# Four row norms transposed and stored at a time, six steps behind their squares, in place of two, three steps behind

## The chip, the core and the metric

The kernel runs on one core of a Trainium2 chip. Its time is the device time of one execution in microseconds (us), the median of three runs. In the text, PE is TensorE (PEld its weight loads), DVE is VectorE, ACT is ScalarE, POOL is GpSimd and SP is SyncE, which here only issues DMA transfers.

## The reference, cut to what matters

One encoder layer for two sequences (1024 and 2048 positions, 1024 features): a gated projection of the input, two kinds of attention side by side, an output projection and a layer norm. The change touches the second kind of attention, in which each head forms two softmax matrices and subtracts one from the other, and whose result is divided by its root mean square:

```python
logits = jnp.einsum('bqhmd,bkhmd->bhmqk', qb, kh).astype(jnp.float32) * (HEAD_DIM ** -0.5)
p = jax.nn.softmax(logits + bias[None, :, None], axis=-1)
w = p[:, :, 0] - lam * p[:, :, 1]
return jnp.einsum('bhqk,bkhe->bqhe', w.astype(vh.dtype), vh)
...
o = rms_norm(o, subln_w) * (1.0 - lambda_init)      # per query and head, over 128 elements
```

There are 4 heads; a block is 128 queries.

## The kernel before, in words

The kernel goes through three stages. Up to about 1150 us it projects the input, with the first kind of attention woven in. From there to about 1822 us runs the stage of the difference attention, called the logits stage here, and after a passage of some 50 us, called the tail, the output projection and the layer norm, which fill PE to the end.

**Slots and steps.** The logits stage has 80 units, one for each block of 128 queries of each head: first 64 of the long sequence (s = 1), then 16 of the short one (s = 0). `slot(n)` works on unit n in four steps, j = 0 to 3. In a step PE does four logits matmuls (L826, into the PSUM tile lg), six value matmuls of an older group (L882 to L884, into ac) and four transposes of an older unit's softmax row (L864, into a PSUM tile tp). The tp tiles come from a pool of two buffers and rotate. DVE adds the bias to the logits and takes the maximum (L831), ACT takes the exponential (L839), POOL subtracts one softmax from the other (L848, L850). Each transposed tile is then copied by ACT (L866, pth) and its remainder formed by DVE (L867, ptl), which also frees the tp buffer. Slots 80 to 85 finish older units while steps of the output projection (a generator, `other`) are woven in; these are the tail.

**Groups and norms.** 256 queries of a head make a group, whose value matmuls, osb copy (L887) and store to `ot` (L888) go together. In the long sequence a unit is a block of 128 queries and a group two units (32 groups); in the short one a unit is a whole group (16 groups). For each group `square_sum` runs at a step j = 1, every second slot in the long sequence and every slot in the short one: two transposes (L897), two squares with sums on ACT (L899), two small DVE operations (L903), and a power of -1/2 on POOL (L905) that leaves the norms of 2 x 128 queries in the tile f. A closure `store` is put on a list. The next step with j = 0, three steps later, takes it from the list behind its four L864: a transpose of f's two columns into a tp tile (L911, two rows), an ACT copy to fr (L913, a pool of one buffer), and a DMA to the DRAM tensor `frow` (L914, on SP's queue). `frow` is read in the output projection alone: `load_rest` loads it back, spread over all partitions, with four other loads for one block (L1029 to L1034, on SP's queue). There are 48 stores, 41 of them in the logits stage and 7 in the tail.

**What sets the order.** In slots below 80 the order on PE is that of the program text, and a scheduler orders the other engines by what is ready. In the tail all engines follow the program text. Each engine works through its own list in order: an instruction that waits holds back all that stands behind it on that engine. POOL also fills the bias window W of the next head (L759), once a head. In the tail ACT issues the stores to `ot` (L888) itself. Eight semaphores are taken in turn by the DMAs of both queues, and a DMA is issued only when the last one of its semaphore has landed; on ACT such a wait holds back all of ACT's list.

Of the kernel before, what the change touches and what calls it, by code (L numbers as in the profile page):

```python
# [11 lines left out]
F32 = mybir.dt.float32  # L12
F32R = mybir.dt.float32r
AF = mybir.ActivationFunctionType
ALU = mybir.AluOpType
# [5 lines left out]
P = 128  # L21
# [46 lines left out]
def hybrid_layer(ctx, tc, x_prompt, x_sample, c_prompt, c_sample, w_in, w_out, w_ada, b_ada, ln_g, ln_b,  # L68
                 attn_sink, lambda_q1, lambda_k1, lambda_q2, lambda_k2, subln_w, rel_bias, oh, eye,
                 y_prompt, y_sample):  # L70
    nc = tc.nc
# [3 lines left out]
    def pool(stack, name, bufs=1, space=None, side=None):  # L75
        if space is None:
            return stack.enter_context(tc.tile_pool(name=name, bufs=bufs, side=side, reuse_waits="tile"))
        if space == DRAM:
            return stack.enter_context(tc.tile_pool(name=name, bufs=bufs, space=space))
        return stack.enter_context(tc.tile_pool(name=name, bufs=bufs, space=space, side=side, reuse_waits="tile"))  # L80
# [6 lines left out]
    def tp():  # L87
        return ps_tp.tile([P, 512], F32, tag="tp", name="tp")

    def ac():  # L90
        return ps_ac.tile([P, 512], F32, tag="ac", name="ac")

    def dt_(shape, name):
        return dram.tile(shape, F32, name=name, tag=name)

    QA, KA, VA, GA, QB, KB, VB, GB, OT, OA = ([] for _ in range(10))
# [13 lines left out]
    frow = [dt_([HB, S], f"frow{s}") for s, S in enumerate(SEQS)]  # L110
    tbl = dt_([HA + HB, P, NREL], "tbl")

    ident = const.tile([P, P], F32, name="ident")
# [3 lines left out]
    mhalf = const.tile([P, 2], F32, name="mhalf")  # L117
# [270 lines left out]
    def fill(n):  # L388
        for _ in range(n):
            next(steps, None)  # L390
# [316 lines left out]
    class Views:  # L707
# [5 lines left out]
        def next(self):  # L713
            if len(self.made) < self.count:
                self.made.append(self.make())
            self.n += 1
            return self.made[(self.n - 1) % self.count]

    SMAX = max(SEQS)
    QG = 256  # L720
# [6 lines left out]
    for s in (1, 0):  # L727
        T = SEQS[s] // P
        for h in range(HB):
            for i in range(0, T, 2):  # L730
                g = len(groups_of)
                n = len(units)
# [6 lines left out]
    N = len(units)  # L739
# [5 lines left out]
    st, lst = ExitStack(), ExitStack()  # L745
# [40 lines left out]
    def prefetch(n, j):  # L786

        s, h, i, g = units[n]
        if j == 1:
            for u in units[n + 1:n + (3 if n >= EARLY - 1 else 2)]:  # L790
                if u[3] == asked[0] + 1 and (u[0] == 0 or u[3] == units[n + 1][3]):
                    load_queries(u[3])
        if n in staged and j == 2:
            stage(staged[n])
        if i == (4 if s else 2) and j == 2 and (s, h) != units[-1][:2]:
            load_head(*next_head[s, h])
        if n + 1 < N and units[n + 1][2] == 0 and j == 3:
            load_keys(*units[n + 1][:2], range(2, SEQS[units[n + 1][0]] // CH))
# [72 lines left out]
    def values(g, piece):  # L871
        s, h, i = groups_of[g]
        T = SEQS[s] // P
        G = groups_[g]
        Vt = heads[s, h][2]
        if piece == 0:
            G["O"] = ac()
        a = G["O"][:, :QG]
        for kb in range(piece * 2, piece * 2 + 2):
            kq, c = divmod(kb, 4)  # L880
            H, L = G["PT"][kq]
            nc.tensor.matmul(a, lhsT=Vt[kq][:, 0, c, :], rhs=H[:, c, :], start=(kb == 0), stop=False)  # L882
            nc.tensor.matmul(a, lhsT=Vt[kq][:, 0, c, :], rhs=L[:, c, :], start=False, stop=False)  # L883
            nc.tensor.matmul(a, lhsT=Vt[kq][:, 1, c, :], rhs=H[:, c, :], start=False, stop=(kb == T - 1))  # L884
        if piece == T // 2 - 1:
            osb = e_p.tile([P, QG], F32, tag="osb", name="osb")
            nc.scalar.copy(osb, a)  # L887
            (nc.sync if now[0] < N else nc.scalar).dma_start(out=OT[s][h][:, i * P:i * P + QG], in_=osb)  # L888
            G["osb"] = osb

    def square_sum(g):
        s, h, i = groups_of[g]
        G = groups_[g]
        ss = st_p.tile([P, 2], F32, tag="ss", name="ss")
        ot = [G["O"][:, QG + b * P:QG + (b + 1) * P] for b in range(2)]
        for b in range(2):
            nc.tensor.transpose(ot[b], G["osb"][:, b * P:(b + 1) * P], ident)  # L897
        for b in range(2):
            nc.scalar.activation(ot[b], ot[b], AF.Square, accum_out=ss[:, b:b + 1])  # L899
        f = st_p.tile([P, 6], F32, tag="f", name="f")  # L900
        nc.scalar.activation(f[:, 0:2], G["s0"], AF.Square, scale=EPS ** 0.5)
        for b in range(2):
            nc.vector.tensor_scalar(out=f[:, 2 + b:3 + b], in0=ss[:, b:b + 1], scalar1=1.0 / P,  # L903
                                    scalar2=f[:, b:b + 1], op0=ALU.mult, op1=ALU.add)
        nc.gpsimd.tensor_tensor(out=f[:, 4:6], in0=f[:, 2:4], in1=mhalf, op=ALU.pow)  # L905
        del groups_[g]

        def store():

            pf = tp()  # L910
            nc.tensor.transpose(pf[0:2, 0:P], f[:, 4:6], ident)  # L911
            fr = f_p.tile([2, P], F32, name="fr")
            nc.scalar.copy(fr, pf[0:2, 0:P])  # L913
            nc.sync.dma_start(out=frow[s][h, i * P:i * P + QG].rearrange("(b p) -> b p", p=P), in_=fr)  # L914

        stores.append(store)

    now, stores = [0], []

    def slot(n, extra, other=None):  # L920
        now[0] = n
        for j in range(4):
            if extra:
                fill(extra)
            if n < N:
                logits(n, j)
                prefetch(n, j)
            for g, piece in values_at.get(n, ()):
                if piece % 4 == j:
                    values(g, piece)  # L930
            if 0 <= n - LAG < N:
                transpose(n - LAG, j)
            if j == 1 and n in sums_at:
                square_sum(sums_at[n])
            if stores and j == 0:
                stores.pop(0)()
            if other is not None:
                next(other, None)

    st_p = pool(st, "stat", 7, side="right")  # L940
# [3 lines left out]
    with tc.manual_schedule(engines={PE}):  # L944
        for n in range(EARLY):
            slot(n, 5)
        project_until(2, 13)
# [2 lines left out]
    v_p = pool(st, "vq", 5)  # L950
    e_p = pool(st, "e", 2)
    f_p = pool(st, "fr", 1)
    for r in (r0_p, r1_p, wb_p, k_p, q_p):
        r.open(st)
    ps_lg.open(lst, space=PSUM)
# [199 lines left out]
    with tc.manual_schedule(engines={PE}):  # L1155
        for n in range(EARLY, N):
            slot(n, 0)
    lst.close()
    ps_po = pool(st, "ps_po", 4, PSUM)
    other = outputs()  # L1160
    with tc.manual_schedule(engines=ENGINES):
        for n in range(N, max(sums_at) + 1):
            slot(n, 0, other)
        for store in stores:
            store()
        for _ in other:
            pass
# [27 lines left out]
```

## Time and profile before

| | us |
|---|---|
| three runs | 2141.43, 2136.42, 2134.31 (median 2136.42) |
| the profiled execution | 2141.53 |
| its span, first to last instruction | 2139.7 |
| PE busy | 2076.0 (97%) |
| POOL, DVE, ACT busy | 1151.5, 1302.1, 1050.5 |

The span is taken from the first to the last instruction; the execution takes 1.8 us longer. The mean clock granted to TensorE was 0.992 of full speed. A row of a timeline gives the start, the duration, the engine, the line, the operation, its output and inputs, shape and count, and in brackets how long the engine sat idle before and which operation released it.

### The profile page before, as it was taken

Reading aid. Unit: us, or ns where it says so; the run is one execution under the profiler, and the core shown is the slowest. Engines: PE = TensorE matmul, PEld = TensorE weight load, DVE = VectorE, ACT = ScalarE, POOL = GpSimd, SP = SyncE. Lnnn points to the kernel's source line nnn. Section 1 sums busy time; section 2 is a strip of 40 time slices with the busy share of each in tenths; the row PEclk is TensorE's granted clock in tenths of the full one; section 3 lists DMA queues with packets and bytes.
Section 4 is the critical chain, followed back from the end, with each engine's and each line's share of the span. In section 5 each row is a group of like instructions: output and inputs, shape, how many; then the busy total and the mean of one; then the engine's idle time right before and its main releaser. Section 6 shows DMA issues by size and latency. Waiting matters only on the chain.

```text
span 2139.7 us, 32697 instructions
## 1 busy us (share of the span) xinstructions
PE 2076.0 (97%) x11645; PEld 1778.9 (83%) x11645; DVE 1302.1 (61%) x2536; ACT 1050.5 (49%) x2070; POOL 1151.5 (54%) x830
## 2 busy tenths in 40 slices
PE   7999999999999999999999999999999999799998
PEld 4777898888988888888887889988888899688886
DVE  5325224212225777677655989989989899555555
ACT  5211103011115677777634777777777799522221
POOL 3213213212124344343344888888888899577774
PEclk9999999999999999999999999999999999899999
DMA  9675635435538868788445122131221362557663
GB/s 271 178 263 176 183 126 167 131 123 136 152 120 228 202 172 212 196 208 213 142 129 156 38 81 77 38 110 50 81 77 38 96 178 90 162 141 204 195 195 102
DMA packets 327338, 312.45 MB, mean 146 GB/s; under 512 B 19126, under 2 KB 284086, under 8 KB 326792
## 3 DMA queue, kind: packets, MB, share of 16 engines
q1 hardware_dynamic: 326456, 309.72, 50.7%
q8 instruction: 92, 1.51, 0.3%
q10 hardware_dynamic: 720, 0.66, 0.1%
q14 instruction: 70, 0.57, 0.1%
HBM read 212.70 MB, written 97.60 MB: 145 GB/s over the span
## 4 chain that ended last, share of the span: by engine, by line
PE 76%; POOL 13%; DMA 4%; DVE 2%; issue 2%; ACT 1%; SPq 1%; ACTq 0%; DVEq 0%; POOLq 0%
PE pj L187 12%; PE pj L188 12%; PE pj L189 12%; PE lg L826 9%; POOL l L850 8%; PE po L1075 4%; PE po L1076 4%; PE po L1077 4%; PE tp L864 4%; POOL l L848 3%; PE lgA L608 3%; PE tp L644 3%; PE ac L882 2%; PE ac L884 2%; PE ac L883 2%; PE ac L636 2%
## 5 line engine op out<-in xcount | busy, mean ns | idle before, releaser
L187 PE MATMUL pj<-uH,wH 128*128 128x512 f32 x1040 | 419.0, 403 | 6.1 <-DVE gg L258 6.1
L189 PE MATMUL pj<-uH,wL 128*128 128x512 f32 x1040 | 407.8, 392 | 0.0
L188 PE MATMUL pj<-uL,wH 128*128 128x512 f32 x1040 | 407.4, 392 | 0.0
L218 POOL TENSOR_TENSOR wL<-wr,wH 128x1024 fp32r<-128x1024 f32 x74 | 181.9, 2460 | 418.8 <-DVE wH L216 377.5
L850 POOL TENSOR_TENSOR l<-l,l 128x1024 f32<-128x1024 f32 x160 | 382.8, 2413 | 1.8
L826 PE MATMUL lg<-kt,Q 128*128 128x512 f32 x1280 | 376.9, 416 | 2.0 <-DVE gg L258 1.4
L839 ACT ACTIVATE l<-l,nm 128x2048 f32<-128x2048 f32 (+1 forms) x192 | 330.7, 1723 | 15.8 <-DVE nm L831 15.8
L866 ACT CAST pth<-tp 128x512 fp32r<-128x512 f32 x320 | 186.2, 582 | 122.1 <-PE tp L864 114.1
L826 PEld LDWEIGHTS lg<-kt,Q 128*128 128x128 f32 x1280 | 217.9, 190 | 32.5 <-DVE nm L831 2.0
L831 DVE CUSTOM_DVE_ANT_0 l<-lg,W 128x1024 f32<-128x1024 f32 x192 | 233.1, 1214 | 11.6 <-PE lg L826 11.5
L848 POOL TENSOR_SCALAR l<-l,s 128x1024 f32<-128x1024 f32 x160 | 179.7, 1136 | 107.0 <-DVE s L844 50.9
L189 PEld LDWEIGHTS pj<-uH,wL 128*128 128x128 f32 x1040 | 195.7, 188 | 42.5
L867 DVE TENSOR_TENSOR ptl<-tp,pth 128x512 fp32r<-128x512 f32 x320 | 212.1, 686 | 28.8 <-ACT pth L866 26.0
L187 PEld LDWEIGHTS pj<-uH,wH 128*128 128x128 f32 x1040 | 196.2, 189 | 39.4 <-DVE gg L258 7.0
L188 PEld LDWEIGHTS pj<-uL,wH 128*128 128x128 f32 x1040 | 196.5, 189 | 31.1
L864 PE MATMUL tp<-ident,l 128*128 128x128 f32 x1280 | 193.5, 274 | 1.6 <-DVE ptl L867 1.4
L623 POOL TENSOR_SCALAR l<-l,rcA 128x384 f32<-128x384 f32 (+1 forms) x144 | 81.4, 584 | 190.6 <-DVE rcA L617 97.2
L882 PE MATMUL ac<-pth,vt 128*128 128x256 f32 x640 | 182.6, 285 | 0.0
L884 PE MATMUL ac<-pth,vt 128*128 128x256 f32 x640 | 181.2, 283 | 0.0
L883 PE MATMUL ac<-ptl,vt 128*128 128x256 f32 x640 | 180.8, 283 | 0.0
L831 DVE CUSTOM_DVE_ANT_0 l<-lg,W,nm 128x1024 f32<-128x1024 f32 x128 | 163.8, 1280 | 24.4 <-PE lg L826 19.9
L864 PEld LDWEIGHTS tp<-ident,l 128*128 128x128 f32 x1280 | 149.0, 141 | 3.9 <-PE lg L826 1.1
(210 smaller groups left out, 4044.7 us busy)
## 6 DMA issues: line engine op xcount, KB each, us to landing
wr<-in_w_in SPq DMA_DIRECT2D x39, 1024.0 KB
KAt<-ka SPq DMA_DIRECT2D x40, 384.0 KB
QAt<-qa SPq DMA_DIRECT2D x24, 512.0 KB
kt<-kb SPq DMA_DIRECT2D x24, 512.0 KB
Q<-qb SPq DMA_DIRECT2D x48, 256.0 KB
Q<-qb SPq DMA_DIRECT2D x96, 128.0 KB
vt<-vb SPq DMA_DIRECT2D x48, 256.0 KB
wa<-in_w_ada SPq DMA_DIRECT2D x32, 256.0 KB
```

The source lines that it names most:

```text
L187: nc.tensor.matmul(acc, lhsT=a(k), rhs=b(k), start=(k == 0), stop=False)
L188: nc.tensor.matmul(acc, lhsT=a(k), rhs=bl(k), start=False, stop=False)
L189: nc.tensor.matmul(acc, lhsT=al(k), rhs=b(k), start=False, stop=(k == KC - 1))
L826: nc.tensor.matmul(L[:, c * CH:(c + 1) * CH], lhsT=G["Q"][:, v, m, b * P:(b + 1) * P], rhs=Kt[kt0 + c][:, m, :], start=(v == 0), stop=(v = ...
L831: nc.vector.tensor_tensor_reduce(out=half, in0=L, in1=W[:, off:off + 1024], scale=1.0, scalar=nm[:, m, 0:1] if s and hf else 3e38, op0=ALU ...
L839: nc.scalar.activation(e, e, AF.Exp, bias=nm[:, m, hf:hf + 1], scale=-1.0, accum_out=sums)
L848: nc.gpsimd.tensor_scalar(out=rows[n][1][:, cs], in0=rows[n][1][:, cs], scalar1=r, scalar2=1.0, op0=ALU.mult, op1=ALU.mult)
L850: nc.gpsimd.tensor_tensor(out=row[:, cs], in0=row[:, cs], in1=rows[n][1][:, cs], op=ALU.add)
L864: nc.tensor.transpose(pt[:, c * P:(c + 1) * P], rows[n][0][:, (j * 4 + c) * P:(j * 4 + c + 1) * P], ident)
L882: nc.tensor.matmul(a, lhsT=Vt[kq][:, 0, c, :], rhs=H[:, c, :], start=(kb == 0), stop=False)
L883: nc.tensor.matmul(a, lhsT=Vt[kq][:, 0, c, :], rhs=L[:, c, :], start=False, stop=False)
L884: nc.tensor.matmul(a, lhsT=Vt[kq][:, 1, c, :], rhs=H[:, c, :], start=False, stop=(kb == T - 1))
```

## The change

The power of -1/2 goes into two of the four columns of a tile `four`, which two neighbouring groups of a head share. Only every second group puts a `store` on the list, with the step at which it falls due: six steps after its squares, which is j = 3 of the next slot. `store` transposes four columns at once, copies four rows and writes 512 contiguous words of `frow`. So 24 transposes, copies and DMAs stand where 48 stood. After the last slot eight steps of the output projection run before the last store. The test for the queue of the `ot` store is rewritten for a counter that counts steps and keeps its meaning. Behind the change the lines are six higher in the output projection (L1029 becomes L1035) and L905, L911, L913, L914 become L909, L915, L917, L918.

```diff
@@ values
-            (nc.sync if now[0] < N else nc.scalar).dma_start(out=OT[s][h][:, i * P:i * P + QG], in_=osb)
+            (nc.sync if now[0] < N * 4 else nc.scalar).dma_start(out=OT[s][h][:, i * P:i * P + QG], in_=osb)
@@ square_sum
-        f = st_p.tile([P, 6], F32, tag="f", name="f")
+        f = st_p.tile([P, 4], F32, tag="f", name="f")
...
-        nc.gpsimd.tensor_tensor(out=f[:, 4:6], in0=f[:, 2:4], in1=mhalf, op=ALU.pow)
+        c = i % 4
+        if c == 0:
+            four[0] = four_p.tile([P, 4], F32, name="four")
+        F = four[0]
+        nc.gpsimd.tensor_tensor(out=F[:, c:c + 2], in0=f[:, 2:4], in1=mhalf, op=ALU.pow)
...
             pf = tp()
-            nc.tensor.transpose(pf[0:2, 0:P], f[:, 4:6], ident)
-            fr = f_p.tile([2, P], F32, name="fr")
-            nc.scalar.copy(fr, pf[0:2, 0:P])
-            nc.sync.dma_start(out=frow[s][h, i * P:i * P + QG].rearrange("(b p) -> b p", p=P), in_=fr)
-
-        stores.append(store)
-
-    now, stores = [0], []
+            nc.tensor.transpose(pf[0:4, 0:P], F, ident)
+            fr = f_p.tile([4, P], F32, name="fr")
+            nc.scalar.copy(fr, pf[0:4, 0:P])
+            nc.sync.dma_start(out=frow[s][h, (i - 2) * P:(i + 2) * P].rearrange("(b p) -> b p", p=P), in_=fr)
+
+        if c:
+            stores.append((now[0] + 6, store))
+
+    now, stores, four = [0], [], [None]
@@ slot
-        now[0] = n
         for j in range(4):
+            now[0] = n * 4 + j
...
-            if stores and j == 0:
-                stores.pop(0)()
+            if stores and stores[0][0] <= now[0]:
+                stores.pop(0)[1]()
...
+    four_p = pool(st, "four", 2)
...
             slot(n, 0, other)
-        for store in stores:
+        for _ in range(8):
+            next(other)
+        for _, store in stores:
             store()
```

PE, the second store of the long sequence. Before, the transpose of f stands behind the L864 of a step j = 0; the waits in brackets name the engines whose semaphores it waits for.

```order
L884 MATMUL ac<-pth,vt 128x256
L864 MATMUL tp<-ident,l_11126 128x128 [waits DVE_49,PE_49,Pool_49]
L864 MATMUL tp<-ident,l_11126 128x128 x3
L911 MATMUL tp<-ident,f 2x128 [waits DVE_49,Pool_49]
L826 MATMUL lg<-kt,Q 128x512 x4
```

In the changed program a transpose of four columns stands behind the L864 of the last step (j = 3) of a slot.

```order
L884 MATMUL ac<-pth,vt 128x256
L864 MATMUL tp<-ident,l_11544 128x128 [waits DVE_49]
L864 MATMUL tp<-ident,l_11544 128x128 x3
L915 MATMUL tp<-ident,four 4x128 [waits DVE_49,PE_49,Pool_49]
L826 MATMUL lg<-kt,Q 128x512 x4
L882 MATMUL ac<-pth,vt 128x256 [waits Activation_49]
```

It has moved from the head of a slot to its end, and both forms wait for DVE as well as for POOL.

DVE, the changed program, an even slot of the long sequence, its steps j = 2 and j = 3 (L831 writes the softmax row l, L841 is a small reciprocal, L867 frees a tp buffer).

```order
L831 ISA l_11428,nm<-lg,W 128x1024
L831 ISA nm 128x1
L841 RECIPROCAL s_11386<-s_11386 128x1
L831 ISA l_11428,nm<-lg,W,nm 128x1024
L831 ISA nm 128x1
L867 TENSOR_TENSOR ptl<-tp,pth 128x4x128 x2
```

The same six rows stand in the program before (l_11434 in place of l_11428); DVE's list has both L867 of the last two steps behind the second L831 there, and what the change adds is a PE instruction that waits for the first of the two.

SP, the queue at the end of the logits stage, before (L1029 to L1034 are the loads of one output block).

```order
L914 DMA frow_102<-fr 2x128
L1029 DMA l_19022<-ot_98 128x4x128
L1030 DMA l_19022<-frow_103 128x4x128
L1031 DMA l_19022<-gb_97 128x4x128
L1032 DMA l_19022<-oa_99 128x4x128
L1034 DMA vt<-in_x_sample 128x1024
L914 DMA frow_102<-fr 2x128
```

And in the changed program:

```order
L918 DMA frow_102<-fr 4x128
L1035 DMA l_18936<-ot_98 128x4x128
L888 DMA ot_81<-osb 128x256
L1036 DMA l_18936<-frow_103 128x4x128
L1037 DMA l_18936<-gb_97 128x4x128
L1038 DMA l_18936<-oa_99 128x4x128
L1040 DMA vt<-in_x_sample 128x1024
L918 DMA frow_102<-fr 4x128
```

The store ahead of the first load is an older one now, and an `ot` store stands behind that load where it stood ahead of the queue's part shown before.

## Rows read from the trace of the kernel before

**Rows 1.** The page's first part: busy time, share of the span and instructions of PE.

```profile
PE 2076.0 (97%) x11645; PEld 1778.9 (83%) x11645; DVE 1302.1 (61%) x2536; ACT 1050.5 (49%) x2070; POOL 1151.5 (54%) x830
```

**Rows 2.** Windows of 50 us: busy time of each engine with its instructions, then the granted TensorE clock, the DMA share and GB/s. The first lies in the logits stage, the second reaches into the tail, the third lies in the output projection.

```profile
1300.00:1350.00 50.00, 49.77 (x336) 44.94 (x335) 45.80 (x88) 39.60 (x67) 42.60 (x26) 1.00 0.20 61
...
1800.00:1850.00 50.00, 42.99 (x293) 39.05 (x292) 39.91 (x80) 40.57 (x100) 38.07 (x27) 0.93 0.38 110
...
2000.00:2050.00 50.00, 50.00 (x217) 40.51 (x217) 27.27 (x47) 12.00 (x19) 37.81 (x33) 1.00 0.65 195
```

**Rows 3.** The timeline of all engines around one regular store of the long sequence (1308 to 1324 us).

```profile
1309.66 4.77 POOL L850 TENSOR_TENSOR l<-l,l 128x1024 f32<-128x1024 f32 x2
...
1312.73 1.18 PE L826 MATMUL lg<-kt,Q 128*128 128x512 f32 x4
...
1314.40 0.69 POOL L905 TENSOR_TENSOR f<-f,mhalf 128x2 f32<-128x2 f32 x1
...
1315.15 0.08 PEld L911 LDWEIGHTS tp<-ident,f 128*2 128x2 f32 x1 [0.33 <-POOL f L905]
...
1315.18 1.18 PE L826 MATMUL lg<-kt,Q 128*128 128x512 f32 x4
...
1317.26 1.18 PE L826 MATMUL lg<-kt,Q 128*128 128x512 f32 x4
```

**Rows 4.** The instructions of line L911 from 1180 to 1820 us: their count, and until what PE or PEld sat idle ahead of them (us, times).

```profile
L911 PE MATMUL tp<-ident,f x41: 270/271/372, 1190.8 to 1815.3; 128*2 128x128 f32 x41
...
  POOL f L905: 31.8, 37
```

**Rows 5.** The instructions of line L914 over the whole span: who waited for them (us, times).

```profile
  ACT fr L913: 5.1, 1
```

**Rows 6.** The timeline of PE around the four latest stores of the logits stage, ahead of each of which POOL had filled W; the last stands at the passage from the long to the short sequence.

```profile
1274.46 1.18 PE L826 MATMUL lg<-kt,Q 128*128 128x512 f32 x4
...
1279.22 0.37 PE L911 MATMUL tp<-ident,f 128*2 128x128 f32 x1 [2.43 <-POOL f L905]
1279.25 2.05 PE L826 MATMUL lg<-kt,Q 128*128 128x512 f32 x4
...
1282.81 1.18 PE L826 MATMUL lg<-kt,Q 128*128 128x512 f32 x4
...
1420.81 0.27 PE L911 MATMUL tp<-ident,f 128*2 128x128 f32 x1 [2.44 <-POOL f L905]
...
1560.64 0.27 PE L911 MATMUL tp<-ident,f 128*2 128x128 f32 x1 [2.19 <-POOL f L905]
...
1701.60 0.27 PE L911 MATMUL tp<-ident,f 128*2 128x128 f32 x1 [3.36 <-POOL f L905]
1701.63 1.41 PE L826 MATMUL lg<-kt,Q 128*128 128x512 f32 x4
...
1704.82 1.61 PE L826 MATMUL lg<-kt,Q 128*128 128x512 f32 x4
```

**Rows 7.** The timeline of all engines at the last step of an even slot of the long sequence and the start of the next slot, where before no store stands.

```profile
1319.35 1.17 PE L826 MATMUL lg<-kt,Q 128*128 128x512 f32 x4
...
1320.56 1.28 DVE L831 CUSTOM_DVE_ANT_0 l<-lg,W,nm 128x1024 f32<-128x1024 f32 x1 [0.17 <-PE lg L826]
...
1321.07 0.60 PE L864 MATMUL tp<-ident,l 128*128 128x128 f32 x4
...
1321.42 1.18 PE L826 MATMUL lg<-kt,Q 128*128 128x512 f32 x4
...
1321.77 1.28 DVE L867 TENSOR_TENSOR ptl<-tp,pth 128x512 fp32r<-128x512 f32 x2
```

**Rows 8.** The timeline of the short sequence: PE around a store of the last slots, and DVE and PE at the last step of a slot.

```profile
1743.59 1.18 PE L826 MATMUL lg<-kt,Q 128*128 128x512 f32 x4
...
1745.77 1.18 PE L826 MATMUL lg<-kt,Q 128*128 128x512 f32 x4
...
1820.62 0.69 DVE L867 TENSOR_TENSOR ptl<-tp,pth 128x512 fp32r<-128x512 f32 x1 [0.17 <-ACT pth L866]
...
1821.45 0.60 PE L864 MATMUL tp<-ident,l 128*128 128x128 f32 x4
```

**Rows 9.** The timeline of SP, ACT and PE in the tail (SPq is SP's queue), in order of time.

```profile
1824.45 0.24 SPq L914 DMA_DIRECT2D frow<-fr  x1
1824.80 0.37 SPq L1029 DMA_DIRECT2D l<-ot  x1
...
1838.37 0.59 ACT L866 CAST pth<-tp 128x512 fp32r<-128x512 f32 x1 [3.56 <-DMA ot<-osb]
...
1839.82 0.37 PE L911 MATMUL tp<-ident,f 128*2 128x128 f32 x1 [3.84 <-DVE ptl L867]
...
1849.60 0.38 SPq L1029 DMA_DIRECT2D l<-ot  x1
...
1862.07 0.72 ACT L1016 ACTIVATE wo<-kt,wsub 128x512 fp32r<-128x512 f32 x1 [8.05 <-DMA l<-gb]
...
1866.74 0.37 PE L911 MATMUL tp<-ident,f 128*2 128x128 f32 x1 [6.49 <-POOL f L905]
...
1872.35 0.27 PE L911 MATMUL tp<-ident,f 128*2 128x128 f32 x1 [1.00 <-POOL f L905]
```

**Rows 10.** The chain that ended last, in the tail: start, duration, what.

```profile
1850.58 11.02 DMA l<-gb
```

## The prediction

> **What bounds the kernel now.** I read the page's busy times first: PE works for 2076.0 us, 97% of the span [rows 1]. The windows say where the rest lies. In a regular stretch of the logits stage PE is busy 49.77 us of 50, in the output projection 50.00, in the window that reaches into the tail 42.99, at a granted clock of 0.93 [rows 2]. So PE bounds the logits stage and the output projection, and the tail is bound by something else. A change to other engines' small work counts only where PE waits for it, or where it adds work to PE.
>
> The timeline shows such a wait. The regular step, from one group of logits matmuls to the next, is 1317.26 - 1315.18 = 2.08 us; the step that ends in a store is 1315.18 - 1312.73 = 2.45 us, 0.37 longer. In front of the store's transpose PE's loads sit idle 0.33 us until POOL has written f [rows 3]. POOL's power starts at 1314.40, when the two L850 before it, 4.77 us long, have left the engine: it is POOL's order that makes f late, not the power's 0.69 us. The instructions of L911 in the logits stage, 41, together saw 31.8 us of such idle time in 37 cases [rows 4]; a long gap stands there once on PE and once on its load side, so I count by steps instead.
>
> **What the change removes.** In the short sequence a store that waits for nothing makes its step 1745.77 - 1743.59 = 2.18 us [rows 8]: 0.10 us is the bare price of a transpose on PE. By steps, the 41 stores of the logits stage cost: 26 regular ones of the long sequence at 0.37, 9.6 us; four late ones, behind a filling of W, with gaps of 2.43, 2.44, 2.19 and 3.36 [rows 6], each with 0.28 around the gap (1279.25 - 1274.46 - 2.08 - 2.43), 11.5 us; eleven of the short sequence at 0.10, 1.1 us. That is 22.2. After two of the four late ones the clock had fallen: the step from 1279.25 to 1282.81 took 3.56, 1.48 too long, that from 1701.63 to 1704.82 took 3.19, 1.11 too long [rows 6]. Together 24.8 us.
>
> Six steps are at least 12.5 us between squares and store instead of 6.2. The latest power came 3.36 us after PE asked for it, so with 6.2 us more it is in time everywhere: none of these waits for POOL is left. The 48 powers on POOL stay, and so does the work on DVE. The copies and DMAs that go cost nothing now: ACT and SP have room, and the only wait that the 48 DMAs caused is one of 5.1 us on ACT in the tail [rows 5]. The Trainium skill ("DMA: Bandwidth & Descriptors", anatomy of one DMA) gives a DMA a fixed cost of about 2.0 us; by it 24 fewer would be worth 48 us if they stood on the path, which the one wait of rows 5 speaks against.
>
> **What it adds.** 20 transposes of four rows in the logits stage at 0.10 each, 2.0 us, as the transpose of two rows: the matrix streamed through PE has 128 columns in both. And a wait that isn't there now. The store takes a tp buffer of the two that rotate. At j = 3 it is the one of step j = 2, and that is free when DVE has done that step's L867. In an even slot of the long sequence the order of DVE has both L867 of j = 2 and j = 3 behind the L831 of j = 3. The rows of such a slot: logits of j = 3 from 1319.35, L831 at 1320.56 for 1.28, the two L867 from 1321.77 for 1.28 together, so the first ends near 1322.43. PE's transposes of j = 3 stand at 1321.07, and the next logits start at 1321.42 [rows 7]: there the store would stand, and would wait from 1321.42 to about 1322.48, 1.05 us. Before, at j = 0, it met a buffer that was long free, and the wait for f hid it. Fourteen of the stores stand at such a place: 14 x 1.05 = 14.7 us. In the short sequence the L867 of j = 2 ends at 1821.31, before the last transposes of j = 3 at 1821.45 [rows 8]: no wait for the other six. Sum of the logits stage: -24.8 + 2.0 + 14.7 = -8 us. The bounds of the wait: nothing, if the scheduler's order or PE's lead differs a little there; up to 1.7, if both L867 must be through.
>
> **The tail.** Two waits of PE stand out, 3.84 us at 1839.82 and 6.49 at 1866.74, both at a store, and 1.00 at 1872.35 [rows 9]. Stores are only the place: the first follows ACT, which held back its copy L866 for 3.56 us until an `ot` store had landed, the second an ACT that stood 8.05 us until the load l<-gb had landed [rows 9], a load that took 11.02 us [rows 10]. These loads are late because SP works in order: the first group of loads starts at 1824.80, right behind the `frow` store of 1824.45, which had waited for its transpose; a later group starts at 1849.60 in the same way [rows 9]. After the change the first group stands behind older stores and can start when the buffer is free, near 1822, about 2.7 us earlier, and the later ones move up with it. The landing times move with the starts, as far as the DMA engines' load allows. So the first wait of PE should lose 2.7 of its 3.84 us, and with it the half clock that follows (I take 1.5 us, as after 1279 [rows 6]); the second should lose about as much as the groups move, 4 to 5 of 6.49, and the third all of its 1.00. That is 2.7 + 1.5 + 4 + 1 = 9 us. Bounds: 3, if only the starved stores themselves go and the landings stay; 12, if all three waits go. Behind the tail PE is full to the end, so what is won there is kept.
>
> Sum: -8 - 9 = -17 us. The profiled execution took 2141.53; its 17 us less are 2124.5. It was the slowest of those shown; against the median of 2136.42 the forecast is 2119.
>
> **The rivals.** *The buffer's wait does not show* (DVE is through in time, or the order differs): the logits stage gives 23 us, the sum is -32, the time 2104 to 2106. For it speaks that DVE is busy 45.80 of 50 us and so has slack [rows 2]; against it that the rows put L867 behind L831 in every even slot.
>
> *The tail gives back little*: the DMA engines are the limit there, the loads start earlier and land no earlier. For it speaks the 11.02 us for a load of 256 KB [rows 10], far longer than its issue; against it that in the window that holds the first of these loads the DMA engines were busy for a share of 0.38 only [rows 2]. Sum -8 - 3 or -8 alone, time 2126 to 2130.
>
> *The new waits cost the clock* (slower). Each of the fourteen is a gap of 1.05 us in a PE that otherwise has none. A gap of 2.43 was followed by a step of 3.56 us, one of 2.44 by none, and the 26 of 0.33 by none [rows 3, 6]. If each of the fourteen were followed by such a step, 1.48 x 14 = 21 us would come on top: +4, 2140; with clock losses over more than one step up to 2.6 each, 36 us: +19, 2156. It decides against the change from 17 / 14 = 1.2 us for each, and shows as slower from 1.7. The Trainium skill ("TensorE: Matmul & The Clock Gate", on a second failure mode, with PSUM buffers cycled) says that frequent short idles of PE between groups of matmuls that cycle through PSUM buffers can make the clock go back and forth, which is this case; the trace's 26 regular gaps do not show it, at a third of the length.
>
> *The waits only change their place*: a PE freed of the waits for f runs into POOL or DVE, so that nothing is won in the logits stage and the tail keeps its path. POOL is busy 42.60 and DVE 45.80 of 50 [rows 2], so there is room for the 8 us; I give it little: time 2132 to 2138.
>
> **How the numbers follow.** The chances: the forecast (2111 to 2126) 0.60, no wait for the buffer 0.10, little from the tail 0.15, the clock 0.08, no gain 0.07. A measurement of this kernel can tell about 0.3% from no change, 6.4 us: faster is below 2130.0, slower above 2142.8. Faster hold the first three, 0.85 less a little for the edge of the third: 0.84. The clock's rival is half between and half above: slower 0.05, the same 0.11. The range 2104 to 2131 holds the first three cases and leaves out the last two, 0.15.
>
> **What would show it.** In the profile of the changed kernel: the idle time in front of L915 released by DVE (L867) and not by POOL, near 1.05 us, fourteen times in the long sequence and next to nothing in the short one; regular steps of 2.08 where L911 stood, and after the fillings of W no gap; the granted clock at 1.00 in the logits stage; the first load of the output projection 2 to 3 us ahead of its old place, the first output matmul about 5 us earlier against the end of the logits stage, and the wait behind the load l<-gb down to one or two us. The prediction is wrong if L915 waits for `four` or for the ACT copy, if the fourteen waits are followed by half-clock matmuls, or if the wait in the tail keeps its length because the transfers and not their starts set it.

## The result, and the profile after

The changed kernel takes 2120.34 us (median; 2118.73 to 2122.41), the kernel before, timed beside it, 2138.13. The ratio is 0.992, with a 95% interval of 0.990 to 0.994: 13 to 22 us faster. The forecast was 2119, range 2104 to 2131.

The windows of the changed kernel answer to [rows 2]; the columns are the same, from the stretch and its length through the busy times of the engines to the granted clock, the DMA share and GB/s.

```profile
1250.00:1300.00 50.00, 49.06 (x335) 44.84 (x335) 45.25 (x87) 38.69 (x64) 43.67 (x28) 1.00 0.42 128
1300.00:1350.00 50.00, 48.14 (x326) 43.71 (x325) 44.87 (x87) 39.14 (x65) 42.90 (x27) 1.00 0.13 41
1790.00:1840.00 50.00, 42.70 (x307) 38.74 (x306) 40.05 (x74) 38.14 (x96) 39.19 (x27) 1.00 0.43 121
1840.00:1865.00 25.00, 21.49 (x96) 17.36 (x95) 9.19 (x18) 7.53 (x22) 16.10 (x15) 0.93 0.52 151
2000.00:2050.00 50.00, 50.00 (x219) 40.75 (x218) 27.54 (x48) 12.07 (x19) 37.77 (x33) 1.00 0.65 192
```

In a window of 50 us that holds one store PE is busy 49.06 us, in one that holds two 48.14; before it was 49.77 in a window without a late store. The output projection is full as it was. The clock stands at 1.00 in the logits stage; the window that reaches into the tail has 1.00 where before it had 0.93, and the 25 us behind it, the tail's end, 0.93.

The timeline of all engines of the changed kernel around a store in an even slot of the long sequence answers to [rows 3, 7]:

```profile
1311.83 1.28 DVE L831 CUSTOM_DVE_ANT_0 l<-lg,W,nm 128x1024 f32<-128x1024 f32 x1 [0.23 <-PE lg L826]
...
1312.34 0.60 PE L864 MATMUL tp<-ident,l 128*128 128x128 f32 x4
...
1313.04 1.28 DVE L867 TENSOR_TENSOR ptl<-tp,pth 128x512 fp32r<-128x512 f32 x2
...
1313.84 0.08 PEld L915 LDWEIGHTS tp<-ident,four 128*4 128x4 f32 x1 [1.14 <-issue]
1313.87 0.27 PE L915 MATMUL tp<-ident,four 128*4 128x128 f32 x1 [0.93 <-DVE ptl L867]
...
1313.89 1.17 PE L826 MATMUL lg<-kt,Q 128*128 128x512 f32 x4
```

The transposes of j = 3 begin at 1312.34 and PE could go on 0.35 us later, as in every step. It goes on at 1313.87, when the first of the two L867 behind the second L831 has ended. The instructions of L915 between 1180 and 1700 us (count; until what PE or PEld sat idle ahead of them, in us and times) answer to [rows 4]:

```profile
L915 PE MATMUL tp<-ident,four x15: 269/269/273, 1209.3 to 1696.2; 128*4 128x128 f32 x15
...
  issue: 16.0, 14
  DVE ptl L867: 13.1, 14
```

POOL no longer stands among the releasers. Fourteen of the fifteen waited for DVE. Counted by steps, each of the fourteen takes 3.27 to 3.28 us against 2.08 for a step without a store, and the others 2.18 to 2.19: 0.10 for the transpose, 1.10 for the wait. In a regular stretch that is a loss, one store at 1.20 us for two at 0.37, as the busy times of the windows show; the logits stage is shorter because the four late waits behind the fillings of W are gone, and the low clock behind them.

Where the time went, by three marks that every kernel here has on PE: the first L897, the last L826, and the fiftieth matmul of the first of the three output lines (L1075 before, L1081 after). The first stretch is the logits stage from its first squares on, the second the tail, the third the output projection. "Median" is the timed one; the stretches are of the one profiled execution.

| kernel | first L897 at | logits stage | tail | rest | median |
|---|---|---|---|---|---|
| before | 1183.8 | 636.7 | 77.7 | 241.6 | 2138.1 |
| before once more (e8) | 1177.0 | 633.9 | 77.6 | 241.6 | 2134.9 |
| changed | 1178.7 | 627.3 | 70.9 | 240.0 | 2120.3 |
| e1 seven steps | 1179.2 | 612.0 | 72.0 | 240.0 | 2104.2 |
| e2 single, six steps | 1179.5 | 644.9 | 74.1 | 240.4 | 2140.8 |
| e3 change in the tail alone | 1179.1 | 632.4 | 71.8 | 240.0 | 2124.4 |
| e4 change in the logits stage alone | 1180.2 | 627.4 | 75.6 | 240.0 | 2124.9 |
| e5 pairs, three steps | 1182.0 | 630.1 | 73.9 | 240.0 | 2126.9 |
| e6 single, seven steps | 1180.1 | 614.2 | 81.6 | 242.1 | 2119.9 |
| e7 seven steps, ot stores on SP | 1177.3 | 612.0 | 62.2 | 240.0 | 2094.3 |
| e9 changed, ot stores on SP | 1176.1 | 627.3 | 63.0 | 240.0 | 2109.9 |
| e10 before, ot stores on SP | 1180.6 | 631.7 | 78.8 | 241.2 | 2134.9 |
| e11 as e10, four places for fr | 1177.7 | 635.3 | 64.9 | 241.2 | 2121.2 |

The kernel before was timed again beside each set of experiments, at 2133 to 2134 us; an experiment's ratio is to that. The changed kernel was not timed again; against these later times its 2120.34 is 13 to 14 us less, and not 18.

The logits stage gave 9.4 us between the two profiles (6.6 against the second profile of before), the tail 6.8, the rest 1.6. The 5.1 us ahead of the first L897 are not the change's (e8 below). Three more kernels have the logits stage of before (e3, e10, e11) and took 632.4, 631.7 and 635.3 us for it, so a stretch of a single profile is good to a few us.

In the tail the changed kernel has these rows in the timelines of SP, ACT and PE, which answer to [rows 9]:

```profile
1807.66 0.37 SPq L1035 DMA_DIRECT2D l<-ot  x1
...
1823.76 0.59 ACT L866 CAST pth<-tp 128x512 fp32r<-128x512 f32 x1 [4.00 <-DMA ot<-osb]
...
1825.12 0.66 PE L864 MATMUL tp<-ident,l 128*128 128x128 f32 x4 [2.84 <-DVE ptl L867]
...
1844.53 0.72 ACT L1022 ACTIVATE wo<-kt,wsub 128x512 fp32r<-128x512 f32 x1 [7.61 <-DMA l<-gb]
...
1847.36 0.69 PE L897 MATMUL ac<-ident,osb 128*128 128x128 f32 x2 [3.51 <-ACT osb L887]
```

Counted from the last L826, which starts at 1820.49 before and at 1806.04 after, the first load comes at 1.6 us where it came at 4.3. But ACT is held 4.00 and 7.61 us where it was held 3.56 and 8.05, each time ahead of an `ot` store that it is to issue (L888). PE's two long waits are 2.84 and 3.51 us in place of 3.84 and 6.49, and neither stands at a store.

The chain that ended last names the transfers that ACT waited for. Before (the second is in [rows 10]):

```profile
1828.36 9.57 DMA ot<-osb
```

And in the changed kernel:

```profile
1813.41 9.90 DMA ot<-osb
...
1833.25 10.82 DMA l<-gb
```

The first is the `ot` store that ACT itself issued before: counted from the last L826 it starts at 7.9 us before and at 7.4 after, and lands at 17.4 and 17.3. The second is a load: it starts at 30.1 and 27.2 and lands at 41.1 and 38.0. So a hold of the same length can end earlier, as the second does.

The tail as one window (from the last L826 to the fiftieth output matmul), before and in the changed kernel:

```profile
1820.49:1898.16 77.67, 63.16 (x346) 53.59 (x345) 40.88 (x68) 34.63 (x91) 49.01 (x40) 0.91 0.54 150
...
1806.04:1876.94 70.90, 60.09 (x343) 51.15 (x342) 40.38 (x68) 33.67 (x88) 49.89 (x40) 0.98 0.58 165
```

PE sits idle for 14.5 us before and for 10.8 after. That is 3.7 of the 6.8 us; the other 3.1 are busy time, of three matmuls fewer at a granted clock of 0.98 in place of 0.91.

### The profile page after: what moved, and what is told of

It reads as the page before. It is cut to its first block, busy times and chain, and to the rows that moved or that the text cites. A ratio compares the mean times of both kernels' runs of the same rounds, so it can differ in the third digit from the quotient of the medians.

```text
span 2116.9 us, 32562 instructions
## 1 busy us (share of the span) xinstructions
PE 2059.4 (97%) x11621; PEld 1769.6 (84%) x11621; DVE 1300.3 (61%) x2536; ACT 1045.9 (49%) x2046; POOL 1151.1 (54%) x830
## 4 chain that ended last, share of the span: by engine, by line
PE 87%; DMA 5%; DVE 4%; ACT 1%; POOL 1%; issue 1%; SPq 1%; ACTq 0%; DVEq 0%; POOLq 0%
PE lg L826 14%; PE pj L187 12%; PE pj L188 12%; PE pj L189 12%; PE tp L864 6%; PE po L1083 4%; PE po L1082 4%; PE po L1081 4%; PE ac L882 3%; PE ac L884 3%; PE ac L883 3%; PE lgA L608 3%; PE tp L644 3%; PE ac L636 2%; PE ac L635 1%; DVE l L831 1%
## 5 line engine op out<-in xcount | busy, mean ns | idle before, releaser
L826 PE MATMUL lg<-kt,Q 128*128 128x512 f32 x1280 | 374.8, 414 | 2.1 <-DVE gg L258 1.4
L839 ACT ACTIVATE l<-l,nm 128x2048 f32<-128x2048 f32 (+1 forms) x192 | 330.9, 1724 | 15.8 <-DVE nm L831 15.8
L831 DVE CUSTOM_DVE_ANT_0 l<-lg,W 128x1024 f32<-128x1024 f32 x192 | 233.5, 1216 | 21.4 <-PE lg L826 21.3
L826 PEld LDWEIGHTS lg<-kt,Q 128*128 128x128 f32 x1280 | 217.1, 189 | 31.9 <-DVE nm L831 2.0
L867 DVE TENSOR_TENSOR ptl<-tp,pth 128x512 fp32r<-128x512 f32 x320 | 210.7, 686 | 17.8 <-ACT pth L866 16.4
L864 PE MATMUL tp<-ident,l 128*128 128x128 f32 x1280 | 192.0, 272 | 5.8 <-DVE ptl L867 5.8
L831 DVE CUSTOM_DVE_ANT_0 l<-lg,W,nm 128x1024 f32<-128x1024 f32 x128 | 164.0, 1281 | 20.9 <-PE lg L826 15.7
L864 PEld LDWEIGHTS tp<-ident,l 128*128 128x128 f32 x1280 | 147.9, 140 | 8.2 <-DVE ptl L867 5.0
```

The lines of the kernel that those rows point to most:

```text
L826: nc.tensor.matmul(L[:, c * CH:(c + 1) * CH], lhsT=G["Q"][:, v, m, b * P:(b + 1) * P], rhs=Kt[kt0 + c][:, m, :], start=(v == 0), stop=(v = ...
L831: nc.vector.tensor_tensor_reduce(out=half, in0=L, in1=W[:, off:off + 1024], scale=1.0, scalar=nm[:, m, 0:1] if s and hf else 3e38, op0=ALU ...
L839: nc.scalar.activation(e, e, AF.Exp, bias=nm[:, m, hf:hf + 1], scale=-1.0, accum_out=sums)
L864: nc.tensor.transpose(pt[:, c * P:(c + 1) * P], rows[n][0][:, (j * 4 + c) * P:(j * 4 + c + 1) * P], ident)
L867: nc.vector.tensor_tensor(out=L[:, :, qs], in0=p3, in1=H[:, :, qs].bitcast(F32), op=ALU.subtract)
```

## The experiments

**e1: one step later.** The store falls due at j = 0 of the slot after, where the buffer of j = 3 is next.

```diff
-            stores.append((now[0] + 6, store))
+            stores.append((now[0] + 7, store))
```

> The changed kernel with the store due seven steps after the squares (j = 0 of the slot after next) in place of six. Theory (the wait of L915 is for the tp buffer of step j = 2, behind DVE's L831): at j = 0 the store takes the buffer of j = 3, whose L867 ends some 0.45 us before; the fourteen steps of 3.28 us become 2.18 each, 14 x 1.1 = 15.4 us less, the time about 2105. Rival (the wait is the price of a transpose of POOL's tile, wherever it stands, or DVE's order follows the store): the steps stay near 3.3 and the time near 2120.

Measured: 2104.18 us, ratio 0.987 (0.985 to 0.989). All 20 steps with a store in the logits stage take 2.18 to 2.19 us. The timeline of all engines around one of them:

```profile
1310.24 1.28 DVE L867 TENSOR_TENSOR ptl<-tp,pth 128x512 fp32r<-128x512 f32 x2
...
1311.62 0.60 PE L864 MATMUL tp<-ident,l 128*128 128x128 f32 x4
...
1312.06 0.27 PE L915 MATMUL tp<-ident,four 128*4 128x128 f32 x1
...
1312.09 1.18 PE L826 MATMUL lg<-kt,Q 128*128 128x512 f32 x4
```

The order of DVE is as before, both L867 behind the L831 of j = 3; they end at 1311.52, the store is reached at 1311.97 and waits for nothing. The logits stage is 15.3 us shorter than the changed kernel's, as the wait for the tp buffer says (14 x 1.1 = 15.4). The time is 16 us lower by the two medians, and 12 by what each is below the kernel before beside it, as the two were timed in different sets.

**e2: the lateness without the pairing.** Each group has its own `four` and a store of two rows, six steps behind its squares.

```diff
         c = i % 4
-        if c == 0:
+        pair = False
+        w = 4 if pair else 2
+        if c == 0 or not pair:
             four[0] = four_p.tile([P, 4], F32, name="four")
         F = four[0]
+        if not pair:
+            c = 0
...
-            nc.tensor.transpose(pf[0:4, 0:P], F, ident)
+            nc.tensor.transpose(pf[0:w, 0:P], F[:, 0:w], ident)
...
-        if c:
+        if c or not pair:
             stores.append((now[0] + 6, store))
```

> The changed kernel without the pairing: 48 stores of two rows, each six steps after its squares. Theory: all stores of the long sequence in the logits stage, about 30, stand at j = 3 of an even slot and wait 1.1 us, twice as many as after the change; some 16 x 1.2 = 19 us more in the logits stage than in the changed kernel, the time about 2139, as slow as before. Rival (the lateness alone is the gain, the pairing saves nothing but 20 x 0.1): about 2123.

Measured: 2140.82 us, ratio 1.0036 (1.0023 to 1.0049): slower than before. The instructions of its store's transpose between 1180 and 1700 us:

```profile
L919 PE MATMUL tp<-ident,four x29: 269/269/273, 1193.3 to 1697.0; 128*2 128x128 f32 x29
...
  DVE ptl L867: 26.2, 28
```

Twenty-eight waits in place of fourteen, each step 3.27 to 3.28 us, and a logits stage 17.6 us longer than the changed kernel's. So the wait costs the same each time, and the lateness alone loses more than the waits for POOL cost: it pays only because the pairing halves its price. The clock does not fall behind any of the 28: the granted clock from 1190 to 1700 us is 1.00.

**e3 and e4: the two halves of the change.** In e3 only the groups of the last two heads of the short sequence are paired and late, in e4 all others; the rest store as before. Both keep the eight output steps ahead of the last store.

```diff
e3, against e2
-        pair = False
+        pair = s == 0 and h >= 2
...
-            stores.append((now[0] + 6, store))
+            stores.append((now[0] + (6 if pair else 3), store))
...
e4, against e3
-        pair = s == 0 and h >= 2
+        pair = s == 1 or h < 2
```

> The kernel before, with pairs and six steps only for the last two heads of the short sequence, whose stores lie in the tail. Theory (the tail's gain comes from its own queue order): the logits stage stays at its 637 us from the first L897 to the last L826, the stretch from the last L826 to the fiftieth output matmul falls from 77.7 to 71 us, the time is about 2131. Rival (the tail gains because of the logits stage ahead of it): 77 us there, the time about 2138.

> The changed kernel with single stores three steps after the squares for the last two heads of the short sequence, as before the change: only the logits stage has pairs. Theory: the logits stage takes 627 us as after the change, the tail to the fiftieth output matmul 77 to 78 as before; the time is about 2127. Rival (the tail follows the logits stage): the tail 71, the time 2120.

Measured: e3 2124.35 us, ratio 0.9956 (0.9940 to 0.9972), 9 us below the kernel before beside it; e4 2124.91, 0.9962 (0.9947 to 0.9977), also 9 us. Added, the halves make 18 us, as the whole did; but that was timed against a slower kernel before (13 to 14 us against the one timed here), and the 1.6 us of the column "rest" are in both halves. So the sum shows that each half gains, and not that nothing else does. The logits stage of e4 is that of the changed kernel (627.4 us), its tail 75.6 us; the tail of e3 is 71.8, near the changed kernel's 70.9. The timeline of PE in the tail of e4 has the two waits of before at their old places, with nearly their old lengths; the third, 1.00 at the last store, is gone, with the eight output steps that e4 keeps:

```profile
1826.78 0.37 PE L919 MATMUL tp<-ident,four 128*2 128x128 f32 x1 [3.75 <-DVE ptl L867]
...
1852.93 0.37 PE L919 MATMUL tp<-ident,four 128*2 128x128 f32 x1 [5.78 <-POOL four L913]
```

e3's time came out 7 us lower than the number expected: the kernel before was itself timed 4.5 us lower in this set, and e3's logits stage was 632.4 us and not 637, as the waits behind the fillings of W differ between executions (e8).

**e5: the pairing without the lateness.**

```diff
-            stores.append((now[0] + 6, store))
+            stores.append((now[0] + 3, store))
```

> The changed kernel with the store of a pair due three steps after the second squares (j = 0 of the next slot), where the stores stood before: pairing without the lateness. Theory: half of the waits for POOL go and half stay, with all four late ones (their groups are second of a pair), and no wait for the tp buffer shows; the steps that hold a store stay at 2.45 to 5.7 us in the long sequence; first L897 to last L826 about 631 us (637 less 15 x 0.37 and 6 x 0.1); the time, with some of the tail's gain, 5 to 9 us below before. Rival (pairing alone takes the wait away): 612 us there.

Measured: 2126.90 us, ratio 0.9965 (0.9951 to 0.9978), a logits stage of 630.1 us: the theory's 631. The steps with a store stay at 2.45 to 2.48 us, the late ones at 3.9 to 6.1; one of these on the timeline of PE:

```profile
1413.58 0.27 PE L915 MATMUL tp<-ident,four 128*4 128x128 f32 x1 [2.56 <-POOL four L909]
1413.61 1.18 PE L826 MATMUL lg<-kt,Q 128*128 128x512 f32 x4
```

The store waits for POOL as before, half as often.

**e6: seven steps without the pairing.** The kernel of e2 with seven in place of six.

```diff
-        stores.append((now[0] + 6, store))
+        stores.append((now[0] + 7, store))
```

> The kernel of e1 (seven steps) without the pairing: 48 stores of two rows. Theory (a store that meets a free buffer and a finished f costs PE its bare 0.10 us): first L897 to last L826 614 us, 2 us above e1, all steps with a store at 2.18; the time 2 to 6 us above e1, the tail with its 7 stores included. Rival (the pairing matters by itself, for copies and DMAs): 10 us or more above e1.

Measured: 2119.91 us, ratio 0.9935 (0.9916 to 0.9955), 16 us above e1. In the logits stage the theory holds: 614.2 us, 2.2 more than e1 for 20 more stores, 0.11 each. So 20 copies and 20 DMAs more cost nothing there. The rest of the difference, 9.6 us in the tail and 2 behind it, was not expected: by its number (10 us or more) the rival is right, in the tail alone. Two of PE's rows and two of ACT's from the timelines of the tail:

```profile
1815.88 0.37 PE L919 MATMUL tp<-ident,four 128*2 128x128 f32 x1 [6.03 <-DVE ptl L867]
...
1814.42 0.59 ACT L866 CAST pth<-tp 128x512 fp32r<-128x512 f32 x1 [5.81 <-DMA ot<-osb]
...
1869.87 0.26 ACT L921 COPY fr<-tp 2x128 f32<-2x128 f32 x1 [15.82 <-DMA frow<-fr]
...
1874.49 0.79 PE L1085 MATMUL po<-W,Q 128*128 128x512 f32 x1 [6.34 <-ACT vt L1125]
```

ACT is held 5.8 us by an `ot` store, and 15.8 us at a copy to fr (L921) until the last `frow` store has left fr. There is one fr, and its store stands on SP's queue behind the loads. Behind the first hold PE waits 6.03 us (2.86 in e1), behind the second 6.34 (none in e1): together 9.5 us more.

**e7: the stores to ot off ACT.** The kernel of e1 with them on SP's queue in the tail as well.

```diff
-            (nc.sync if now[0] < N * 4 else nc.scalar).dma_start(out=OT[s][h][:, i * P:i * P + QG], in_=osb)
+            nc.sync.dma_start(out=OT[s][h][:, i * P:i * P + QG], in_=osb)
```

> The kernel of e1 with the stores to ot issued on SP's queue in the tail too, in place of ACT's. Theory (what starves PE in the tail is ACT held back by such a store, 3.9 and 7.7 us): both holds leave ACT, PE's waits of 2.9 and 3.6 us shrink, the stretch from the last L826 to the fiftieth output matmul falls from 72 to about 67 us and the time by 3 to 5 us against e1. Rival (SP held by the same wait keeps back the loads behind it): 72 us or more and no gain.

Measured: 2094.30 us, ratio 0.981 (0.980 to 0.983), 10 us below e1, twice what was expected, with a tail of 62.2 us. Of the 9.8 us that the tail is shorter than e1's, 6.8 are idle time of PE (3.6 in place of 10.4); the rest is busy time, at a granted clock of 1.00 in place of 0.95 over the tail. PE's longest wait in it on PE's timeline is this one, which the kernels with ACT's stores have too:

```profile
1796.27 0.66 PE L864 MATMUL tp<-ident,l 128*128 128x128 f32 x4 [1.05 <-DVE ptl L867]
```

This is the fastest version.

**e8: the kernel before once more.** No edit.

> The kernel before once more, for a second profile. Theory (the first 5 us of the difference between the two profiles, ahead of the first L897, is no effect of the change): first L897 at 1179 to 1180 us as in all changed kernels; the gaps ahead of the four late stores differ between executions by up to 1.5 us, first L897 to last L826 632 to 637 us. Rival: first L897 at 1184 again.

Measured: 2134.93 us, ratio 1.0003 (0.9992 to 1.0013). The first L897 comes at 1177.0, and in all other profiles at 1176.1 to 1182.0: the 5 us ahead of it differ between executions and are no effect of the change. The steps with the late stores take 4.30, 4.09, 3.84 and 5.92 us where the first profile had 4.79, 4.79, 4.54 and 5.72. The instructions of L911 between 1170 and 1815 us:

```profile
  POOL f L905: 27.0, 34
```

That was 31.8 in [rows 4]. By steps, the 41 with a store in the logits stage take 105.8 us here and 108.2 there, which is most of the 2.8 us between the two logits stages.

**e9 and e10: what the tail's gain rests on.** The edit of e7 in the changed kernel (e9) and in the kernel before (e10).

> The changed kernel (six steps) with the stores to ot on SP's queue in the tail too. Theory (the holds of ACT at these stores starve PE in the tail, and the logits stage is independent): the stretch from the last L826 to the fiftieth output matmul falls from 70.9 us to 61 to 63, the logits stage stays at 627; the time about 2110, 10 us below the changed kernel. Rival (the gain of e7 needs the store at seven steps): 70 us, 2119.

> The kernel before with the stores to ot on SP's queue in the tail too. Theory (the change's gain in the tail is a shorter effect of the same holds of ACT): the tail falls from 77.6 us to about 64 to 67, at most 4 us more than in e9, so that of the change's 7 us there half or more is gone; the time about 2122. Rival (the change's gain in the tail comes from its fewer stores, their buffer and their queue, apart from ACT's holds): the tail stays 7 us or more above e9's, 69 us or more.

Measured: e9 2109.91 us, ratio 0.990 (0.987 to 0.992), tail 63.0, as expected. e10 2134.90, ratio 1.0007 (0.9993 to 1.0022), tail 78.8: in the kernel before the same edit gains nothing. My theory falls and the rival's number holds; the holds of ACT at the `ot` stores are not all. The timelines of ACT and PE in e10:

```profile
1860.87 0.26 ACT L913 COPY fr<-tp 2x128 f32<-2x128 f32 x1 [10.88 <-DMA frow<-fr]
...
1863.10 0.37 PE L911 MATMUL tp<-ident,f 128*2 128x128 f32 x1 [9.70 <-POOL f L905]
```

With the holds at L888 gone ACT waits 10.88 us at a copy to fr until the `frow` store before has landed, the squares behind the copy are late, and PE waits 9.70 us at the next store.

**e11: more places for fr, in e10.** Four groups of partitions of one tile take the two rows in turn. (A pool of four tiles for fr has no room: it leaves 14.9 KB per partition for the pool `late`, which takes 16.)

```diff
-            fr = f_p.tile([2, P], F32, name="fr")
+            k = 32 * (turns[0] % 4)
+            turns[0] += 1
+            if turns[1] is None:
+                turns[1] = f_p.tile([P, P], F32, name="fr")
+            fr = turns[1][k:k + 2]
...
-    now, stores = [0], []
+    now, stores, turns = [0], [], [0, None]
```

> The kernel of e10 (before, with the stores to ot on SP's queue) with the copies to fr going to four places in turn (four groups of partitions of one tile) in place of one. Theory (in e10 PE's wait of 9.7 us at 1863 comes from ACT, which held its copy to fr for 10.9 us until the last frow store had left the only buffer, a store that stands behind the loads on SP's queue): the copies no longer wait for the store before, the wait of 9.7 us falls to 1 us or less, the stretch from the last L826 to the fiftieth output matmul falls from 78.8 us to about 70 and the time to about 2126. Rival (the wait is for the store's data or its place, not for the buffer): 78 us, 2135.

Measured: 2121.24 us, ratio 0.994 (0.992 to 0.996), tail 64.9, 5 us below what was expected. The timelines of PE and ACT at the last store:

```profile
1852.04 0.27 PE L911 MATMUL tp<-ident,f 128*2 128x128 f32 x1 [0.17 <-POOL f L905]
...
1852.35 0.26 ACT L917 COPY fr<-tp 2x128 f32<-2x128 f32 x1 [1.50 <-PE tp L911]
```

The wait of 9.70 us is 0.17, ACT's copy waits for the transpose alone. Without pairs and without lateness the tail comes within 2 us of e9's. So two causes hold ACT in the tail of the kernel before, the `ot` stores and the single fr. As it stands the second holds it for 5.1 us only ([rows 5]); with the first alone taken away it holds it for 10.88, and the tail stays at 79 us. The second alone was not tried.

## Why the prediction was right, and where it was not

**What the change removes** held. Behind it no store of the long sequence waits for POOL; e5, where they stay without the lateness, and e2, where its 28 waits are for DVE, show that it was the lateness that took them away. The size, 24.8 us, came from a single execution: the second profile of before has shorter late waits (e8), and its logits stage is 2.8 us shorter.

**What it adds** held nearly to the digit: fourteen waits for the L867 of j = 2, forecast at 1.05 us and measured at 1.10, none in the short sequence as far as it lies in the logits stage. e1 shows that the buffer makes the wait, since one step later the wait is gone with DVE's order as it was, and e2 that it costs the same each time. The logits stage was to give 8 us; it gave 9.4 and 6.6 against the two profiles of before, and 4.4 to 8.0 against the three others with the same logits stage.

**The tail** was forecast at -9; the traces give 6.8 there and 1.6 more behind it, and no term but the last has the size forecast. The step that failed is the first wait. It was to lose 2.7 us because the loads start 2.7 us earlier, and they did (1.6 us behind the last L826 and not 4.3). But this wait does not hang on the loads' start: it hangs on the `ot` store that ACT had issued before, which starts 0.5 us earlier and lands at 17.3 us in place of 17.4. With these stores off ACT (e9) no wait of PE at this place is over 0.3 us. Why such a store takes 9.6 to 9.9 us no run shows. The wait lost 1.0 us all the same. Before, it stood at a store, which itself takes a tp buffer, right behind the four L864; after, no store stands there, and PE gets through six value matmuls more before it meets the buffer that is held. I read that from the rows; no run takes it apart.

The second wait, 6.49, lost 3.0 (4 to 5 forecast), and here "the landing times move with the starts" held: the load l<-gb starts 2.9 us earlier, takes 10.8 us for 11.0, and the hold ends 3.1 us earlier. Before, PE took up its work 5.1 us behind that end, at a store that waited for f, whose squares ACT had late; that store is now one with the last, behind eight output steps, and PE goes on 3.2 us behind it, at L897. But PE also reaches the place 1.95 us earlier: 3.08 + 1.85 - 1.95 = 2.98. The 1.00 at the last store went as forecast. The smaller waits grew by 1.3 us, which the prediction does not have; the two largest new ones are 1.05 and 1.04 us, both for L867. So the waits gave 3.7 us where 7.7 were forecast.

The clock gave more than its 1.5: PE's busy time fell by 3.1 us. That hangs on the execution. In the changed kernel's profile the clock did not fall behind the first wait; in e3, whose tail has the same stores, it did behind a wait of 3.12 us, and PE was idle for 9.6 us of its tail and busy for 62.2, at a clock of 0.93. Two of the signs asked for also failed: the first output matmul comes 2.7 us earlier against the end of the logits stage and not 5, and the wait behind l<-gb is 3.51 us and not one or two.

Half the number of stores matters too, which the prediction left at "cost nothing": with the single fr and SP's order, 48 stores keep ACT waiting in the tail (e6, e10), and e11 shows that it is the fr buffer. The tails of e4, e2 and e5 (75.6, 74.1 and 73.9 us, with the eight output steps alone, with them and the lateness, with them and the pairs) against 70.9 with all three suggest that each has a share; with a clock that differs from profile to profile they do not measure it.

**The sum** came out nearer than its terms, and that is luck in part: of the 17.8 us against 17 forecast, some 4 are the slow timing of the kernel before in that set and 1.6 come from the output projection, which no term foresaw.

**The rivals.** The buffer's wait shows, so the first falls. The second (little from the tail) was right about the first wait, whose transfer lands only 0.2 us earlier, and wrong about the second; its time, 2126 to 2130, did not come. The third, that the new waits cost the clock, falls: fourteen waits of 1.1 us, and 28 in e2, pass at a granted clock of 1.00 (the level of 2.4 GHz), each with a following step of full speed. The rule of the Trainium skill ("TensorE: Matmul & The Clock Gate", on a second failure mode) does not show here at such gaps. That the waits only change their place was true of the fourteen, at three quarters of the old price: 15.4 us where the waits for POOL and the clock behind them had cost 20.7 (the 24.8 less 41 transposes at 0.10).

## What to carry to other kernels

A small operation that takes a buffer of a short rotation waits for the buffer's last reader, however early its own data is: before it is moved, ask which buffer it will draw at the new place and what stands in front of the reader that frees it. Here six steps gained 18 us and seven 29 (e1), each against the kernel before timed beside it. Where an engine issues DMAs or fills a single buffer that a DMA empties, count its holds one after the other: taking one away gained nothing (e10), taking both away 13 us (e11).

## What the runs showed that I had not expected

The output projection runs the same matmuls at a slightly different rate: from the fiftieth to the hundredth of the first line 34.74 us in both profiles of before and in e10 and e11, 34.56 in the changed kernel and in e1 to e5, e7 and e9. PE is fully busy in both, at a clock of 1.00. Over the whole output projection that makes some 1.2 us, most of the 1.2 to 1.6 us of the column "rest". The kernels of the second kind have a pool more and a smaller f, so other tiles may lie elsewhere in memory; that was not tried, and the cause stays open.
